# A state-space stage on one core, its hand-written order of operations sorted anew

## The chip, the cores and the metric

The kernel runs on one core of one Trainium2 chip. The metric is device time in microseconds (us), the median of the runs. Lines (L531) are those of the kernel's source. Engines: PE is TensorE (PEld its weight loads), DVE VectorE, ACT ScalarE, POOL GpSimd, SP SyncE, which here only issues DMAs.

## What is computed

A trunk of two layers on x (1 x 512 x 1024, float32): one state-space layer with a GLU and an MLP with squared ReLU, then shared keys, values and forget gates, one attention layer, a second MLP and a final norm. Only the first part matters here:

```python
def s5_mixer(u, log_dt, a_re, a_im, b_re, b_im, c_re, c_im, d_skip, w_glu):
    ...
    lam = lax.complex(a_re.astype(f32), a_im.astype(f32))
    dt = jnp.exp(log_dt.astype(f32))[:, None]
    lam_bar = jnp.exp(lam * dt)
    b = lax.complex(b_re.astype(f32), b_im.astype(f32))
    b_bar = ((lam_bar - 1.0) / lam)[..., None] * b
    bu = jnp.einsum('blgc,gpc->blgp', uf.astype(jnp.complex64), b_bar)
    a_elems = jnp.broadcast_to(lam_bar, bu.shape)
    _, states = lax.associative_scan(_ssm_binop, (a_elems, bu), axis=1)
    c = lax.complex(c_re.astype(f32), c_im.astype(f32))
    y = jnp.real(jnp.einsum('blgp,gcp->blgc', states, c))
    y = y + d_skip.astype(f32).reshape(N_GROUPS, SSM_GROUP) * uf
    z = jax.nn.gelu(y.reshape(bsz, length, D_MODEL)).astype(u.dtype)
    zw = z @ w_glu
    val, gate = zw[..., :D_MODEL], zw[..., D_MODEL:]
    return val * jax.nn.sigmoid(gate)
```

There are 64 groups of 16 channels with 64 complex states each.

## The kernel before

The sequence is cut into 64 chunks of T = 8 tokens, the 64 groups into 8 blocks of 8 groups. For each block b the kernel makes two weight matrices, runs the scan over the chunks, and adds a Toeplitz product for what happens inside a chunk. The operations have short names, and a string, ORDER (L37), lists them as name_block; a loop at L745 to 748 calls them in that order. The whole stage lies in a manual schedule over all five engines (L174), so each engine, SP and POOL with their DMA queues too, takes its own instructions exactly in the order of the string. An engine whose next instruction waits stands still, and so does all that is queued behind it.

The operations of a block, with the engine that runs each:

- win1, win2 (DVE, L531 and L536): two multiplies of 128 x 1024. wina (POOL, L345): an accumulating DMA of 512 KB adds the second onto the first (tile Win). wo1, wo2, woa: the same for the output weights (tile TW). win2 and wo2 need XY with its halves swapped, which sw does (SP, two DMAs, L341 and L342). gR and a gain on POOL (L460) scale XY first.
- pw (PE, L580): Win transposed; wt (ACT, L353): copied out of PSUM as WinT.
- u (PE, L564): the scaled input transposed; us (ACT, L353): copied to Uall. xs (ACT, L552) scales the input, after rxv (DVE) has made the norm's factor.
- pt (PE, L591): the taps, Win times Wout; ks (ACT): copied; kd (DVE, L603): the skip weight added; kw (SP, L607): written to DRAM; tr (SP, L613): read back, 512 KB, as a Toeplitz matrix, into the second half of TW.
- tab0 (DVE, L362), tab3 (ACT, L368 to L373, six instructions): tables of cosine and sine.
- pd (PE, L627): input to the states; ds, cos (DVE, L637 and L633): rotation; da (POOL): two accumulating DMAs of 128 KB onto cc; scan (DVE, L647; its factors from dec, ACT and POOL); P1, P2 (DVE, L655 and L652): rotation back; padd (POOL): two accumulating DMAs of 128 KB.
- py1 (PE, L663): Toeplitz part, needs tr; py2 (PE, L663): state part, needs padd and Wout. gelu (ACT, L678), zt (PE, L684), zh (ACT), lo (DVE, L697): activation, transpose, and a split into a high and a low part for the GLU.
- gl (SP, L113), gs (ACT, L124), gv (DVE, L128): load and split of a piece of w_glu; gp (PE, L731): six matmuls of the GLU. The rest of the GLU (L810) comes behind the stage.
- Once each: kz, dl, gnl (SP: zeros, and gains; gnl loads the four norm gains that gn transposes on PE), tk, ta, dg (DVE).

Buffers tie the blocks together. TW lives in slots of a pool with two tags, A and B, of two buffers each; the string WQ says which tag each new TW, and then gs_2 and gs_1, takes. A slot is free again only when py2 of the block that had it is done, so the wo1 of a later block waits for the py2 of an earlier one. Win has three buffers, tB two for each kind, PSUM eight of one bank (pool ps), used by pw (2), pt (2), pd, py, zt, u and each started GLU chunk (2).

```python
            for o in ORDER.split():
                f, *args = o.split("_")
                e = {"V": {"e": V}, "G": {"e": G}, "S": {"e": S}}.get(f[-1], {}) if f not in OPS else {}
                OPS[f[:-1] if e else f](*map(int, args), **e)
```

The old order works on the blocks as 0, 1, 2 and 4, 3, 5, 7, 6; block 6 is the last whose tables (tab3_6) and reload (tr_6) are made. At the start it does sw, the multiplies of blocks 0 to 2 and two loads of w_glu ahead of gnl, and the first wina is behind woa_1 on POOL.

Of the kernel before, what the change touches and what calls it, by code (L numbers as in the profile page):

```python
# [32 lines left out]
MAGIC = 12582912.0  # L33
TWO_PI = 2.0 * math.pi
CFG = dict(seq=['sfoqlantpx', 'soflntapxq'], pat=[2, 1, 1, 1, 1, 1, 1, 1, 1, 1, 1, 1, 1, 1, 1, 1, 1, 1, 1, 1, 1, 1, 1, 1, 1, 1, 1, 1, 1, 1, 1, 1, 1, 1, 0, 2, 1, 1, 1, 1, 1, 1, 1, 1, 1, 1, 1, 1, 1, 1, 1, 1, 1, 1, 1, 1, 1, 1, 1, 1, 1, 1, 2, 1, 1, 1], nl=4, nt=1, u0=66, ns=[], wk=4, st=['f u02 u03 u10 u11 u12 s u13 c0 c1', 't t u02 f t u03 u10 u11 t u12 u13 s c0 c1'], x='GGGGGGGGGGVbb', m0=3)
WQ = "AABBBABABA"
ORDER = """  # L37
LR mR dl_0 kz gR dl_1 rxv decS_0 sw_2_0 sw_2_1 win1V_2 xsS_0_1 gl_1 win1V_0 gl_2 xsS_1_0 sw_0_1 wo2V_0 gnl
wo2V_1 xsS_1_1 win2V_1 gl_0 xsS_0_0 tk u_3 u_6 u_2 taV gn usS_6 u_0 tab0V_0 usS_3 u_1 tab0V_2 usS_0 u_4
tab0V_1 u_5 tab3_2 u_7 wo1V_1 win2V_0 woa_1 wo1V_4 wina_0 usS_5 win1V_1 usS_4 tab3_0 wo1V_2 wina_1 wo1V_0  # L40
wo2V_3 woa_0 pw_0 win2V_4 usS_7 usS_1 dg wtS_0 pt_1 win2V_2 tab3_1 tab0V_3 wina_2 pw_1 tab0V_4 wo2V_2 pt_0
win1V_5 woa_2 wtS_1 pd_0 win1V_4 ksS_0 tab0V_5 wina_4 pd_1 ksS_1 ds_0 cos_0 tab3_3 kd_0 da_0 pw_2 cos_1 kw_0
wo2V_4 pt_2 kd_1 woa_4 win2V_3 kw_1 tr_0 pw_4 wtS_2 win1V_3 scan_0 wina_3 wtS_4 tr_1 P1V_0 decS_1 pd_4 ds_1
ksS_2 P2V_0 da_1 py1_0 tab3_4 wo2V_7 padd_0 kd_2 pt_4 win2V_5 kw_2 win2V_7 wina_5 py1_1 ksS_4 ds_4 tr_2 pw_3
cos_4 usS_2 kd_4 da_4 scan_1 gs_0 pd_2 tab3_5 P1V_1 P2V_1 py2_0 cos_2 padd_1 gv_0 kw_4 py1_2 wo1V_3 gelu_0
pw_5 ds_2 woa_3 tr_4 win2V_6 decS_2 da_2 zt_0 py2_1 zhS_0 win1V_7 wtS_5 lo_0 wina_7 gelu_1 pd_5 wo1V_5 wtS_3
scan_2 zt_1 py1_4 zhS_1 P2V_2 P1V_2 decS_4 pd_3 lo_1 padd_2 scan_4 pw_7 decS_3 P1V_4 pt_3 P2V_4 wtS_7 ds_3
padd_4 cos_3 gp_0_0 ksS_3 cos_5 da_3 kd_3 gp_0_1 wo2V_5 kw_3 win1V_6 py2_2 woa_5 tab0V_7 wina_6 tr_3 pd_7
gelu_2 wo1V_6 tab3_7 ds_5 zt_2 py2_4 scan_3 da_5 P1V_3 pt_5 P2V_3 wo1V_7 padd_3 py1_3 ksS_5 ds_7 woa_7 zhS_2
kd_5 pw_6 cos_7 kw_5 decS_5 da_7 lo_2 wtS_6 py2_3 scan_5 tr_5 gelu_4 pd_6 P2V_5 P1V_5 gelu_3 wo2V_6 padd_5  # L50
zt_4 gs_2 zt_3 tab0V_6 pt_7 zhS_3 woa_6 gv_2 zhS_4 py1_5 lo_3 ksS_7 lo_4 gp_0_2 tab3_6 kd_7 kw_7 gp_0_3 py2_5
tr_7 pt_6 gelu_5 ds_6 gp_2_0 cos_6 da_6 gp_2_1 gs_1 ksS_6 gv_1 zt_5 gp_2_3 zhS_5 kd_6 kw_6 gp_1_0 decS_6 lo_5
scan_6 gp_1_2 tr_6 P2V_6 decS_7 gp_1_1 P1V_6 gp_2_2 padd_6 scan_7 py1_7 P2V_7 P1V_7 py1_6 padd_7 gp_1_3 py2_6
py2_7 gelu_6 zt_6 gelu_7 zhS_6 zt_7 lo_6 zhS_7 lo_7
"""


def body(tc, x, mix_norm, mlp_norm, mlp_w1, mlp_w2, log_dt, a_re, a_im, b_re, b_im,
# [4 lines left out]
    with ExitStack() as ctx:  # L63
# [74 lines left out]
        with ExitStack() as s5c:  # L138
# [374 lines left out]
            W, glu = {}, {}  # L513
            wqk = iter(WQ)

# [1053 lines left out]
```

## Time and profile before

| | |
|---|---|
| median of 3 runs | 1218.62 us (1217.38 to 1219.13) |
| profiled execution | 1225.04 us, span of the core's instructions 1223.3 us |
| PE busy | 1123.5 us (92%), PEld 1000.2 us (82%) |
| DVE busy | 913.9 us (75%) |
| ACT busy | 610.2 us (50%) |
| POOL busy | 295.5 us (24%) |
| granted TensorE clock, mean | 0.968 |
| DMA queues, share of 16 engines | SP's 32.5%, POOL's 6.1% |

Busy shares are means over the whole span; the stage that the change touches is the first seventh of it. The profiled execution is 1.7 us longer than its span. Times in the rows are us from the span's start.

### The profile page before, as it was taken

What the parts mean: (1) busy time and instruction counts of PE and PEld (TensorE: products, weight loads), DVE (VectorE), ACT (ScalarE), POOL (GpSimd) and SP (SyncE); (2) the same over time, 40 slices, a digit from 0 to 9 for tenths busy, and PEclk for the clock granted to TensorE, in tenths of its full rate; (3) what the DMA queues carried; (4) which work ended last, traced back from release to release, by engine and by line L of the source; (5) the groups of instructions that cost most, each with busy time, mean ns of one, the idle gap of its engine ahead of it and who ended that gap; (6) DMA issues with size and microseconds to landing.
All of it is one profiled execution on the core that took longest, in us unless ns stands there. A gap on an engine that the chain in (4) does not pass through costs nothing.

```text
span 1223.3 us, 19032 instructions
## 1 busy us (share of the span) xinstructions
PE 1123.5 (92%) x7189; PEld 1000.2 (82%) x7189; DVE 913.9 (75%) x1639; ACT 610.2 (50%) x1108; POOL 295.5 (24%) x298
## 2 busy tenths in 40 slices
PE   1467789999999999999999999888899999999997
PEld 1456678899898999988888999867799999898986
DVE  8766546879977787777755788884999877778754
ACT  5673736545444344434544666553664434344433
POOL 5133313422212212110302222222422121212101
PEclk9977889999999999999999999898899999999999
DMA  6887864314323232334235433421133323323222
GB/s 136 182 172 130 157 148 130 102 53 138 121 87 121 87 120 88 103 105 123 70 103 139 105 104 104 121 70 35 52 111 114 120 87 108 100 90 113 82 97 69
DMA packets 109388, 131.37 MB, mean 107 GB/s; under 512 B 9360, under 2 KB 87984, under 8 KB 109296
## 3 DMA queue, kind: packets, MB, share of 16 engines
q1 hardware_dynamic: 104432, 117.57, 32.5%
q0 software_dynamic: 4864, 12.59, 6.1%
q8 instruction: 57, 0.93, 0.3%
q14 instruction: 35, 0.29, 0.1%
HBM read 103.21 MB, written 2.74 MB: 87 GB/s over the span
## 4 chain that ended last, share of the span: by engine, by line
PE 79%; DMA 7%; DVE 6%; ACT 4%; issue 2%; SPq 2%; POOL 1%; DVEq 0%; ACTq 0%; POOLq 0%
PE pu L919 26%; PE po L810 15%; PE pvs L1484 14%; PE pk L810 6%; PE pv L810 5%; DMA TW<-kd 3%; PE pvs L1130 2%; PE po L1268 2%; DMA kd<-ks 1%; PE pt L591 1%; PE pf L1118 1%; PE ptp L1234 1%; DMA bc<-in_ssm_b_im_dram 1%; DVE prob L1229 1%; PE pd L627 1%
## 5 line engine op out<-in xcount | busy, mean ns | idle before, releaser
L919 PE MATMUL pu<-hm,ar 128*128 128x256 f32 x1536 | 229.8, 285 | 3.2 <-ACT hm L863 2.2
L919 PEld LDWEIGHTS pu<-hm,ar 128*128 128x128 f32 x1536 | 205.3, 194 | 4.5 <-ACT hm L863 2.6
L124 ACT ACTIVATE wt<-st 128x1024 fp32r<-128x1024 f32 x110 | 116.3, 1057 | 129.3 <-PE po L810 30.5
L810 PE MATMUL po<-at,wt 128*128 128x512 f32 x768 | 176.9, 389 | 0.0
L898 POOL TENSOR_TENSOR ar<-ar,st 128x256 f32<-128x256 f32 x62 | 72.6, 1173 | 429.7 <-DVE ar L894 400.5
L1484 PE MATMUL pvs<-wt,at 128*128 128x512 f32 (+1 forms) x768 | 175.5, 388 | 0.0
L810 PEld LDWEIGHTS po<-at,wt 128*128 128x128 f32 x768 | 143.2, 188 | 29.1
L1484 PEld LDWEIGHTS pvs<-wt,at 128*128 128x128 f32 x768 | 142.6, 188 | 28.8
L128 DVE TENSOR_TENSOR wt<-st,wt 128x1024 fp32r<-128x1024 f32 x90 | 117.2, 1303 | 35.4 <-ACT wt L124 35.4
L919 PE MATMUL pu<-hd,x 128*128 128x256 f32 x768 | 137.0, 286 | 0.0
L887 ACT ACTIVATE ar<-ar 128x512 fp32r<-128x512 f32 x128 | 77.0, 627 | 92.2 <-PE pu L919 84.7
L919 PEld LDWEIGHTS pu<-hd,x 128*128 128x128 f32 x768 | 114.2, 194 | 2.7 <-issue 0.5
L888 DVE TENSOR_TENSOR ar<-ar 128x512 fp32r<-128x512 f32 x128 | 87.9, 692 | 31.4 <-ACT ar L887 31.4
L887 ACT ACTIVATE x<-st 128x512 fp32r<-128x512 f32 x62 | 36.2, 624 | 98.3 <-PE pvs L1484 49.7
L128 POOL TENSOR_TENSOR wt<-st,wt 128x1024 fp32r<-128x1024 f32 x20 | 48.1, 2407 | 145.3 <-ACT wt L124 127.2
L894 DVE TENSOR_TENSOR ar<-st 128x512 f32<-128x512 f32 x62 | 52.0, 841 | 32.8 <-DMA st<-in_mlp_w_dram 32.1
L810 PE MATMUL pv<-zt,wt 128*128 128x512 f32 x312 | 72.9, 392 | 0.3 <-ACT hT L992 0.3
L810 PEld LDWEIGHTS pv<-zt,wt 128*128 128x128 f32 x312 | 58.0, 188 | 12.4 <-ACT hT L992 0.6
L1220 ACT ACTIVATE prob<-psx,mx 128x128 f32<-128x128 f32 (+1 forms) x64 | 33.8, 528 | 60.9 <-DVE mx L1218 60.9
L899 POOL TENSOR_TENSOR ar<-ar,st 128x256 f32<-128x256 f32 x62 | 60.3, 975 | 4.2
L1039 ACT ACTIVATE at<-c 128x512 fp32r<-128x512 f32 x64 | 39.7, 630 | 40.4 <-DVE c L1037 40.4
L1025 DVE TENSOR_TENSOR hT<-hT,po 128x512 f32<-128x512 f32 x64 | 43.4, 679 | 14.8 <-PE po L810 14.8
(333 smaller groups left out, 2057.0 us busy)
## 6 DMA issues: line engine op xcount, KB each, us to landing
st<-in_mlp_w_dram SPq DMA_DIRECT2D x126, 512.0 KB, 3.5
st<-in_ssm_w_glu_dram SPq DMA_DIRECT2D x16, 512.0 KB, 6.7
st<-in_w_kvf_dram SPq DMA_DIRECT2D x14, 512.0 KB, 3.6
hx<-kt SPq DMA_DIRECT2D x48, 128.0 KB, 2.3
TW<-tB POOLq DMA_DIRECT2D x8, 512.0 KB, 6.4
Win<-tB POOLq DMA_DIRECT2D x8, 512.0 KB, 9.2
TW<-kd SPq DMA_DIRECT2D x8, 512.0 KB
st<-in_attn_wq_dram SPq DMA_DIRECT2D x8, 512.0 KB, 3.4
```

Of the source, the lines that this page charges most:

```text
L124: S.activation(wt[:, 0], st, AF.Copy)
L128: (G if slot[1] == "A" and CFG["x"][7 + lows[0] % 3] == "G" else V).tensor_tensor(wt[:, 1], st, wt[:, 0].bitcast(F32), op=ALU.subtract)
L810: TE.matmul(pts[m], wt[:, a, k, m * P:(m + 1) * P], acts[k0 + k][:, b], start=(first and k0 == parts[0][0] and k == 0 and n == 0), stop=(k ...
L887: S.activation(X[0], src, AF.Copy)
L888: V.tensor_tensor(X[1], src, X[0].bitcast(F32), op=ALU.subtract)
L894: V.tensor_tensor(Ta[:, :, js].rearrange("p w j n -> p j w n"), f[:, :, 1:3], f[:, :, 0:1].broadcast_to([P, 2, 2, P]), op=ALU.add)
L898: e.tensor_tensor(Tb[:, 0, js], Ta[:, 0, js], v[:, :, 1, 0], op=ALU.add)
L899: e.tensor_tensor(Tb[:, 1, js], Tb[:, 0, js], v[:, :, 1, 1], op=ALU.add)
L919: TE.matmul(self.acc[p], self.W[p][:, a, j], self.H.moving(p, j, b), start=(p == g[0] and j == 0 and n == 0), stop=(p == g[-1] and j == 3 ...
L1025: V.tensor_tensor(hT[:, m, :], hT[:, m, :], po[j], op=ALU.add)
L1039: S.activation(at_[:, 0], c, AF.Square)
L1484: TE.matmul(po[:, cols], A[k][:, b], wts[k // 2][:, a, k % 2, cols], start=start and n == 0, stop=stop and n == 3 * len(ks) - 1)
```

## The change

The string ORDER is replaced by another arrangement of the same operations, each of them once, and WQ by another row of the same ten letters. Nothing else differs. In the new order kz and gnl come first on SP, win2_0, win1_0 and wina_0 first on DVE and POOL, and the blocks go 0 to 7 in their own order (with small exchanges of neighbours, such as wt_5 ahead of wt_4). All tables are made by the time of ks_4; usS_6 and usS_7 come just ahead of tab3_5; the last block is 7 in every kind of operation. On DVE, 11 multiplies and 3 table adds come ahead of cos_0 and ds_0.

```diff
-WQ = "AABBBABABA"
+WQ = "AABBABABAB"
-LR mR dl_0 kz gR dl_1 rxv decS_0 sw_2_0 sw_2_1 win1V_2 xsS_0_1 gl_1 win1V_0 gl_2 xsS_1_0 sw_0_1 wo2V_0 gnl
-wo2V_1 xsS_1_1 win2V_1 gl_0 xsS_0_0 tk u_3 u_6 u_2 taV gn usS_6 u_0 tab0V_0 usS_3 u_1 tab0V_2 usS_0 u_4
-tab0V_1 u_5 tab3_2 u_7 wo1V_1 win2V_0 woa_1 wo1V_4 wina_0 usS_5 win1V_1 usS_4 tab3_0 wo1V_2 wina_1 wo1V_0
-wo2V_3 woa_0 pw_0 win2V_4 usS_7 usS_1 dg wtS_0 pt_1 win2V_2 tab3_1 tab0V_3 wina_2 pw_1 tab0V_4 wo2V_2 pt_0
-win1V_5 woa_2 wtS_1 pd_0 win1V_4 ksS_0 tab0V_5 wina_4 pd_1 ksS_1 ds_0 cos_0 tab3_3 kd_0 da_0 pw_2 cos_1 kw_0
-wo2V_4 pt_2 kd_1 woa_4 win2V_3 kw_1 tr_0 pw_4 wtS_2 win1V_3 scan_0 wina_3 wtS_4 tr_1 P1V_0 decS_1 pd_4 ds_1
-ksS_2 P2V_0 da_1 py1_0 tab3_4 wo2V_7 padd_0 kd_2 pt_4 win2V_5 kw_2 win2V_7 wina_5 py1_1 ksS_4 ds_4 tr_2 pw_3
-cos_4 usS_2 kd_4 da_4 scan_1 gs_0 pd_2 tab3_5 P1V_1 P2V_1 py2_0 cos_2 padd_1 gv_0 kw_4 py1_2 wo1V_3 gelu_0
-pw_5 ds_2 woa_3 tr_4 win2V_6 decS_2 da_2 zt_0 py2_1 zhS_0 win1V_7 wtS_5 lo_0 wina_7 gelu_1 pd_5 wo1V_5 wtS_3
-scan_2 zt_1 py1_4 zhS_1 P2V_2 P1V_2 decS_4 pd_3 lo_1 padd_2 scan_4 pw_7 decS_3 P1V_4 pt_3 P2V_4 wtS_7 ds_3
-padd_4 cos_3 gp_0_0 ksS_3 cos_5 da_3 kd_3 gp_0_1 wo2V_5 kw_3 win1V_6 py2_2 woa_5 tab0V_7 wina_6 tr_3 pd_7
-gelu_2 wo1V_6 tab3_7 ds_5 zt_2 py2_4 scan_3 da_5 P1V_3 pt_5 P2V_3 wo1V_7 padd_3 py1_3 ksS_5 ds_7 woa_7 zhS_2
-kd_5 pw_6 cos_7 kw_5 decS_5 da_7 lo_2 wtS_6 py2_3 scan_5 tr_5 gelu_4 pd_6 P2V_5 P1V_5 gelu_3 wo2V_6 padd_5
-zt_4 gs_2 zt_3 tab0V_6 pt_7 zhS_3 woa_6 gv_2 zhS_4 py1_5 lo_3 ksS_7 lo_4 gp_0_2 tab3_6 kd_7 kw_7 gp_0_3 py2_5
-tr_7 pt_6 gelu_5 ds_6 gp_2_0 cos_6 da_6 gp_2_1 gs_1 ksS_6 gv_1 zt_5 gp_2_3 zhS_5 kd_6 kw_6 gp_1_0 decS_6 lo_5
-scan_6 gp_1_2 tr_6 P2V_6 decS_7 gp_1_1 P1V_6 gp_2_2 padd_6 scan_7 py1_7 P2V_7 P1V_7 py1_6 padd_7 gp_1_3 py2_6
-py2_7 gelu_6 zt_6 gelu_7 zhS_6 zt_7 lo_6 zhS_7 lo_7
+LR mR kz gnl win2V_0 win1V_0 decS_0 dl_1 rxv wina_0 gl_1 sw_2_0 gn win2V_1 xsS_1_1 dl_0 gR sw_2_1 xsS_0_1 tk
+sw_0_1 wo2V_0 gl_2 xsS_1_0 gl_0 pw_0 wo2V_1 wo1V_0 u_3 wtS_0 u_6 dg u_2 xsS_0_0 woa_0 u_7 wo1V_2 wo1V_1 usS_2
+u_5 u_0 usS_5 taV woa_1 u_1 usS_0 u_4 tab0V_2 usS_1 pd_0 tab0V_0 usS_4 gs_0 tab0V_1 win1V_1 tab3_0 pt_0 wo2V_2
+wina_1 gv_0 woa_2 win2V_3 ksS_0 cos_0 tab3_2 ds_0 kd_0 da_0 wo2V_4 kw_0 win1V_3 pw_1 win1V_2 wina_3 tab3_1
+pt_1 win2V_2 wo2V_3 wina_2 tab0V_3 scan_0 wtS_1 tr_0 pd_1 P1V_0 decS_1 P2V_0 ksS_1 wo1V_3 padd_0 pw_3 tab3_3
+ds_1 cos_1 woa_3 kd_1 win1V_5 kw_1 pw_2 da_1 win2V_4 usS_3 wtS_2 pt_2 win2V_5 wtS_3 tab0V_7 wina_5 py1_0
+win1V_4 ksS_2 tab0V_5 wina_4 py2_0 tab3_7 kd_2 tab0V_4 kw_2 wo2V_5 pd_2 tr_1 wo1V_4 pd_3 ds_2 woa_4 gelu_0
+scan_1 pt_3 cos_2 decS_2 cos_3 da_2 tab3_4 zt_0 P2V_1 pw_5 win1V_6 win2V_6 tr_2 P1V_1 wina_6 tab0V_6 padd_1
+win2V_7 zhS_0 ksS_3 lo_0 wtS_5 py1_1 kd_3 kw_3 wo2V_6 tab3_6 pw_4 ds_3 pd_5 scan_2 da_3 P1V_2 wtS_4 py1_2
+P2V_2 decS_3 padd_2 pd_4 usS_6 usS_7 tab3_5 pt_4 cos_4 tr_3 py2_1 win1V_7 wina_7 pw_6 ds_4 ksS_4 wo1V_5 da_4
+py2_2 wtS_6 kd_4 scan_3 kw_4 gelu_1 woa_5 pd_6 P1V_3 P2V_3 gelu_2 zt_1 cos_5 padd_3 py1_3 zhS_1 wo1V_6 decS_4
+lo_1 pw_7 woa_6 gp_0_0 wtS_7 ds_5 tr_4 scan_4 da_5 pd_7 P1V_4 decS_5 gp_0_1 P2V_4 cos_6 padd_4 pt_5 wo2V_7
+zt_2 ksS_5 py2_3 zhS_2 kd_5 kw_5 pt_6 wo1V_7 gelu_3 lo_2 woa_7 zt_3 ksS_6 py1_4 zhS_3 kd_6 kw_6 ds_6 lo_3 da_6
+py2_4 scan_5 tr_5 gp_0_3 gelu_4 P2V_5 gs_2 P1V_5 pt_7 cos_7 padd_5 decS_6 gv_2 tr_6 zt_4 ksS_7 gp_2_0 zhS_4
+kd_7 ds_7 gp_2_1 da_7 lo_4 gp_2_3 kw_7 scan_6 py1_5 P1V_6 decS_7 P2V_6 py2_5 padd_6 py1_6 gelu_5 gs_1 scan_7
+zt_5 tr_7 gp_2_2 zhS_5 gv_1 gp_0_2 P2V_7 P1V_7 gp_1_0 lo_5 padd_7 py2_6 gp_1_2 gelu_6 zt_6 py1_7 zhS_6 lo_6
+gp_1_1 py2_7 gp_1_3 gelu_7 zt_7 zhS_7 lo_7
```

## Rows read from the trace of the kernel before

**Rows 1.** Busy time of each engine by stretch: busy (x), granted clock, DMA share, GB/s.

```profile
core 0: us, PE busy (x) PEld busy (x) DVE busy (x) ACT busy (x) POOL busy (x), PEclk, DMA share, GB/s
32.00:175.00 143.00, 98.36 (x995) 83.87 (x996) 87.34 (x111) 81.06 (x127) 41.32 (x55) 0.86 0.79 155
64.00:90.00 26.00, 15.76 (x154) 13.91 (x154) 15.59 (x22) 19.11 (x30) 10.32 (x14) 0.74 0.92 175
175.00:252.00 77.00, 76.74 (x364) 63.90 (x363) 52.35 (x61) 41.86 (x69) 25.14 (x23) 1.00 0.39 124
252.00:1223.00 971.00, 943.40 (x5796) 848.08 (x5794) 748.38 (x1366) 469.95 (x878) 213.04 (x177) 0.98 0.32 98
```

**Rows 2.** Chain of waits, end of the stage: start, us, what.

```profile
153.79 5.42 DMA kd<-ks
...
159.27 7.87 DMA TW<-kd
...
167.28 1.97 PE py L663 x32
...
174.72 2.27 PE pv L810 x9
...
196.04 50.16 PE pv L810 x220
```

**Rows 3.** Groups of instructions, 0 to 180 us: busy us, mean ns, idle before.

```profile
L591 PE MATMUL pt<-TW,Win 128*16 128x128 f32 x128 | 19.7, 321 | 2.3 <-DMA TW<-tB 1.7 <-ACT cs L372 0.5
L731 PE MATMUL pv<-zt,wt 128*128 128x512 f32 x72 | 19.2, 420 | 0.0
L627 PE MATMUL pd<-Uall,WinT 128*128 128x64 f32 x128 | 18.9, 312 | 2.0 <-ACT WinT L353 2.0
L663 PE MATMUL py<-TW,Uall 128*64 128x64 f32 x256 | 12.5, 270 | 24.3 <-DMA TW<-kd 24.3
L580 PE MATMUL pw<-ident,Win 128*128 128x128 f32 x64 | 10.8, 325 | 4.0 <-ACT cs L368 3.0 <-DMA Win<-tB 1.0
L531 DVE TENSOR_TENSOR TW<-LL,XY 128x1024 f32<-128x1024 f32 x8 | 9.8, 1221 | 1.8 <-PE pu L564 1.6 <-PE py L663 0.2
L353 ACT ACTIVATE ks<-pt 16x512 f32<-16x512 f32 x16 | 9.0, 582 | 8.3 <-PE pt L591 8.2
L678 ACT ACT_TABLE_LOAD x3 | 3.8, 1283 | 0.1
L372 ACT ACT_TABLE_LOAD x2 | 2.6, 1283 | 0.0
```

**Rows 4.** Timeline of SP: start us, us, engine and line, what.

```profile
26.15 0.52 SPq L341 DMA_DIRECT2D XY<-XY  x1
...
30.95 0.53 SPq L341 DMA_DIRECT2D XY<-XY  x1
```

**Rows 5.** Timeline of the other engines up to 84 us, same columns, idle before.

```profile
34.27 2.36 DVE L536 TENSOR_TENSOR tB<-LL,XY 128x1024 f32<-128x1024 f32 x2 [3.77 <-DMA XY<-XY]
44.28 0.86 POOL L345 DMA_DIRECT2D Win<-tB  x1
62.65 0.69 DVE L637 SCALAR_TENSOR_TENSOR dt<-pd,cs 128x512 f32<-128x512 f32 x1 [0.17 <-PE pd L627]
72.88 0.63 ACT L368 ACTIVATE cs<-cs 128x512 f32<-128x512 f32 x1
...
76.01 0.80 ACT L373 ACTIVATE cs<-cs,sg 128x512 f32<-128x512 f32 x1
83.08 0.57 ACT L353 ACTIVATE Uall<-pu 128x512 f32<-128x512 f32 x1
```

**Rows 6.** Timeline of DVE and PE, 119 to 163 us.

```profile
120.14 1.23 DVE L531 TENSOR_TENSOR TW<-LL,XY 128x1024 f32<-128x1024 f32 x1 [0.20 <-PE py L663]
...
124.36 1.22 DVE L531 TENSOR_TENSOR TW<-LL,XY 128x1024 f32<-128x1024 f32 x1
161.71 1.15 PE L663 MATMUL py<-TW,Uall 128*64 128x64 f32 x32
```

**Rows 7.** DMA issues of the page: KB each, median us from issue to landing.

```profile
TW<-tB POOLq DMA_DIRECT2D x8, 512.0 KB, 6.4
```

## The prediction, made before the changed kernel ran

> **What bounds the kernel now.** I read first how busy each engine is, stretch by stretch, then the chain of waits, then the timeline of the first 175 us, which is all that the change touches. From 175 us to 252 us PE is busy 76.74 of 77 us (the GLU's matmuls), and from there to the end 943 of 971 us [rows 1]. So the second part is PE's own length, and what the state-space stage gains or loses reaches the end one for one. In the stage itself nothing is full: from 32 to 175 us PE is busy 98 of 143 us, DVE 87, ACT 81, POOL 41, and the DMA engines 0.79, with 0.92 in the best stretch [rows 1]. A stage in which every resource has room is bound by waits, and the order decides the waits. The chain shows the last of them: kd at 153.79 takes 5.42 us to DRAM, the Toeplitz reload 7.87 us, py1_6 starts at 167.28, and the GLU's own matmuls begin at 174.72 [rows 2]. This was block 6, whose tables, kernel taps and reload the old order does last of all, after block 7's.
>
> **What the change does.** It adds and drops no operation: 12 GLU pieces, 16 accumulating DMAs of 512 KB, 8 reloads on both sides. The letters of WQ follow the new order of the Wout tiles: nothing by themselves. Two ACT table loads may go: ACT now switches between Sin and Gelu five times [rows 3], in the new order three times (gelu_0, back for tab3_4, gelu_1), 2 x 1.28 us. They are inside the sum of ACT below.
>
> **Start.** SP must first wait for POOL's gain; it issues the first swap at 26.15, and a swap was waited for 3.3 us after its issue (30.95 to 34.27) [rows 4, 5]. win2V_0, now at the head of DVE, so starts at 29.5 (bounds: a landing of 2 to 6 us, 28 to 32). Two multiplies later (1.22 us each [rows 3]) POOL issues wina_0, at 31.9 instead of 44.28 [rows 5]: the first transfer of the blocks starts 12 us earlier. What that costs: rxv, and with it the 16 xs copies on ACT, wait behind these multiplies. That is covered, because before the Uall copies had to wait on gn anyway, whose loads SP issued after the swaps and two w_glu loads; now gnl is ahead of all but kz. Without that cover it costs the 6 us or so by which rxv moves.
>
> **First scan input.** Before, ds_0 starts at 62.65 [rows 5]. The new DVE queue has 6 multiplies fewer ahead of it (7.3 us), 3 table adds of half that size fewer (1.8 us), and gv_0 more (1.2 us): 54.8 with the old waits, 51 without any. I take 53.5, with ACT's tab3_0 just done.
>
> **Middle.** From there ACT holds the pace. Until wtS_4 its queue has 6 tab3 at 3.9 us (72.88 to 76.81 [rows 5]), 23.4; four ks and five wt at 1.2 (two copies each, like those of ks [rows 3]), 10.8; dec_1, dec_2, us_3, gelu_0 and zh_0 at about 0.7, 3.6; two table loads, 2.6. Sum 40.4, done at 93.9. PE then does pd_4, pt_4 and py2_1: 2.4, 2.5 and 1.6 (busy time of each group divided by 8 blocks [rows 3]), 6.5: 100.4. That frees a slot for wo1V_5. From py2_1 to py2_3 PE's queue holds two pw (1.4 each), two pd (4.7), one pt (2.5), two gp (3.2), three py (4.7) and two zt (0.7 each, half a pw): 19.3. At 119.7 py2_3 frees the slot for wo1V_7, which ran at 124.36 before [rows 6].
>
> **Last block.** From wo1V_7 the chain is woa_7, pt_7, ks_7, kd_7, kw_7, tr_7, py1_7: 37.35 us before (124.36 to 161.71 [rows 6]). The parts alone are woa at 6.4 [rows 7], pt 2.5, ks 1.2, kw 5.42 and the reload 7.87 [rows 2]: 23.4 us. The old lap also held woa_7 in POOL's queue behind other transfers and kw_7 behind ACT's tab3_6 path; in the new order all tables are done by then. I take 33, nearer the measured lap than the bare parts. After it come py1_7, one gp and py2_7, 4.8 us (block 6 no longer stands between). End of the stage: 119.7 + 33 + 4.8 = 157.5 instead of 174.72, **17 us less**. With 23.4 it is 27 us, with 37.35 it is 13.
>
> **The DMA queue as a check.** From 32 to 175 us the DMA engines worked 0.79 x 143 = 113 us [rows 1]. The new order starts at about 32 too: at 0.92 it cannot end before 155, at 0.90 it ends at 157.5, at 0.79 at 175. So 17 us need the best stretch's density all along; this caps the gain at 20 us or so, and is where it can be lost.
>
> POOL's 512 KB took 6.4 us in the median from issue to landing [rows 7]. The Trainium skill (DMA: Bandwidth & Descriptors, Anatomy of one DMA) gives such a DMA about 2 us plus its bytes over 436 GB/s; an estimate from that page is 3.2 us for woa and for the reload and 2.2 for kw. By it the bare parts would be 12 us, the end at 137 and the gain 38 us. The row decides against it.
>
> **Waits that are new.** On POOL, da_2 stands behind the memset of dec_2, which on ACT stands behind gelu_0, which needs py2_0; wina_6, padd_1 and da_3 queue behind it. py2_0 follows padd_0 and tr_0; with ds_0 at 53.5 and kd_0 just after it, kw_0 and tr_0 (5.42 and 7.87) end near 68 and py2_0 near 72, while ACT comes to gelu_0 near 75: 3 us of cover, and beyond it ACT and POOL lose one for one. On SP, tr_1 stands behind kw_2, and tr_5 behind kw_6. tr_1 then goes out near 73 and lands near 81; py1_1 comes after pw_5 on PE, about 79, so 2 us may be lost there, which the wait for wtS_4 hides.
>
> **Behind the stage.** SP, POOL and the GLU's weight loads keep their work; DMA share there is 0.39 [rows 1], so the weights come in time for a GLU that starts earlier, and PE has no room there to lose the gain. The profiled execution took 1225.04 us, 6.4 above the median of the runs; I take the 17 us off the median, 1218.62: **1201 us**.
>
> **Rivals.**
> 1. The DMA engines are the bound. For it: the share of 0.92 at 64 to 90 us [rows 1], where DVE and PE had room. Moving wina_0 forward puts it beside the w_glu loads, and woa, wina, da and padd share POOL's one queue. (The Trainium skill, the same page, Issuing engines are not separate DMA queues: transfers that SP and POOL issue run on the same 16 engines and interleave. The trace agrees as far as 0.92 goes.) At a share of 0.83 the stage ends at 32 + 113 / 0.83 = 168: 7 us less, 1212.
> 2. It changes nothing that can be measured: 0.79 is what these transfers reach with such latencies, and the end stays at 175. A measurement of this kernel tells about 0.2% (2.4 us) from no change. 1218.6.
> 3. It is slower: PSUM. The pool has 8 buffers. The new order transposes u_6 and u_7 early on PE and copies them (usS_6, usS_7) only behind tab3_6, wtS_4 and decS_3, past 90 us by the ACT sum; before, one such buffer stayed that long (copied at 83.08 [rows 5]). Six buffers then serve pw (2), pt (2), pd, py and zt, and gp_0, which holds two, comes 13 us earlier. If PE stands still for a buffer that ACT frees only behind a wait for PE, each lap of a slot grows. The old order's longest, wo1V_6 at 120.14 to 174.72, is 54.6 us [rows 2, 6]; with the early lead eaten (wo1V_7 at 124.4) the stage ends at 179 and the kernel at 1223. It decides once py1_1 starts later than about 100 us.
> 4. More than I think: the lap near its bare 23.4 us, 1191.
>
> **Chances.** My forecast (1192 to 1208) 0.57; rival 1 (1208 to 1216) 0.19; rival 2 0.07; rival 3 0.13; rival 4 (under 1192) 0.04. Faster by over 0.2%: 0.80; within: 0.07; slower: 0.13. The range runs from just above the short lap, 1192, through rival 1 and a little into no change, 1217; it leaves out rivals 3 and 4 and about half of rival 2.
>
> **What would show it.** Right: wina_0 issued near 32, the first dt near 53 to 55, ACT's last tab3 before 100, wo1V_7 (the last TW multiply) between 113 and 122, py1_7 the last reload's reader, and PE's first GLU matmul outside the stage (line 810) near 157. Two ACT table loads fewer. From there to the end the same length as before. Wrong: a first dt after 60; idle time of PE in front of pw, pt or py put down to an ACT copy (rival 3); or scans idle behind the cc transfers with a DMA share over 0.9 and an end past 165 (rival 1).

## The result, and the profile after

The changed kernel took 1204.69 us in the median of 10 runs (1199.35 to 1211.47), the kernel before 1219.66 in 10 runs beside them (1213.08 to 1228.59): ratio 0.9869, 95% interval 0.9837 to 0.9901. A second measurement, beside other runs of before, gave 0.9876 (0.983 to 0.9922). Forecast were 17 us less; by these ratios it was 15 to 16. The medians differ by 15.0 and 14.7 us.

The profiled execution of the changed kernel took 1199.35 us (span 1197.6), the shortest of its ten runs, while that of before, 1225.04, lies near the top of what that kernel's ten runs span. The two traces therefore differ by more than the medians, and I keep to what they show about places. Busy time by stretch, in the columns of [rows 1]:

```profile
core 0: us, PE busy (x) PEld busy (x) DVE busy (x) ACT busy (x) POOL busy (x), PEclk, DMA share, GB/s
32.00:158.00 126.00, 102.06 (x1024) 87.83 (x1025) 88.58 (x113) 83.55 (x132) 40.42 (x54) 0.85 0.84 173
64.00:90.00 26.00, 20.57 (x243) 18.53 (x242) 19.47 (x26) 23.91 (x38) 8.71 (x12) 0.83 0.96 183
158.00:235.00 77.00, 75.85 (x380) 63.96 (x378) 54.49 (x64) 42.57 (x73) 30.49 (x28) 1.00 0.36 113
235.00:1197.00 962.00, 935.79 (x5751) 840.41 (x5749) 741.30 (x1360) 465.73 (x869) 207.68 (x172) 0.99 0.33 99
```

The stage holds the same work in less time: PE is busy 102 of 126 us, where it was 98 of 143. Behind it hardly anything has changed. From the start of the long run of 220 GLU matmuls to the end of the span it is 1025.2 us here and 1027.3 before [rows 2]; in all 14 profiles of this study it lies between 1022.8 and 1027.7. The start of that run is therefore my measure of the stage: 172.43 instead of 196.04.

What PE waited for from 30 to 155 us (in all, how often, the longest):

```profile
engine line waited for: us in total, times, longest us
PE pw L580 <- DMA Win<-tB: 11.3, 2, 8.2
PE py L663 <- ACT ks L353: 5.4, 1, 5.4
PE py L663 <- DMA P<-P: 5.2, 2, 3.2
PE pw L580 <- ACT Uall L353: 2.2, 1, 2.2
PE pd L627 <- ACT WinT L353: 2.1, 1, 2.1
PE pt L591 <- DMA TW<-tB: 2.1, 2, 1.2
PE py L663 <- DMA TW<-kd: 1.5, 1, 1.5
```

The last line is the one to see. Before, PE stood 24.3 us in front of py1 because the Toeplitz reload TW<-kd had not landed [rows 3]; now 1.5. The reload of block 6 is no faster (10.52 us below, 7.87 before [rows 2]). What changed is the distance: from a block's kd to its py1 it is 14.5 to 24.1 us now and was 10.9 to 19.7, longer for every block, and the string puts 92 operations of PE between pt and py1, summed over the blocks, where it put 70. Block 0 is the exception: it has six on both sides. Its wait of 6.36 us for the reload is gone too, but PE now waits 3.06, 2.13 and 2.20 us in front of pw_1, pd_1 and pw_2, which stand between its pt and its py1.

The reloads are not the whole difference. All of PE's waits from 30 to 182 us add up to 51.4 us before and 30.0 now, 21.4 less. Two more waits of the kernel before, both at the start, are gone (its profile, same window):

```profile
PE pg L705 <- DMA gl<-in_mlp_norm_dram: 9.3, 1, 9.3
PE pu L564 <- ACT xs L552: 8.0, 1, 8.0
```

In their place PE waits 8.2 us for the Win of block 0 (pw_0), and the waits for ACT's ks and for P are new or longer.

The timeline of the places that the forecast named (wina_0, ds_0, the end of tab3_6 and wt_4, py2_1, wo1_7, py1_7):

```profile
27.84 1.06 POOL L345 DMA_DIRECT2D Win<-tB  x1 [1.57 <-DVE rxa L486]
...
47.54 0.68 DVE L637 SCALAR_TENSOR_TENSOR dt<-pd,cs 128x512 f32<-128x512 f32 x1
...
86.06 0.80 ACT L373 ACTIVATE cs<-cs,sg 128x512 f32<-128x512 f32 x1
86.76 1.05 ACT L353 ACTIVATE WinT<-pw 128x512 f32<-128x512 f32 x2
...
92.40 1.15 PE L663 MATMUL py<-TW,P 128*64 128x64 f32 x32
...
115.64 1.23 DVE L531 TENSOR_TENSOR TW<-LL,XY 128x1024 f32<-128x1024 f32 x1 [0.78 <-PE py L663]
...
149.21 1.15 PE L663 MATMUL py<-TW,Uall 128*64 128x64 f32 x32
```

And the end of the chain of waits (start, us, what):

```profile
117.16 5.24 DMA TW<-tB
...
124.14 10.52 DMA TW<-kd
...
134.79 1.98 PE py L663 x32
...
146.12 2.72 PE pv L810 x12
...
149.28 1.08 PE py L663 x32
...
154.61 3.63 PE pv L810 x16
...
172.43 50.16 PE pv L810 x220
```

woa_7 lands, the reload of block 6 follows, and py1_6 at 134.79 is PE's last wait of the stage. From there PE works without a gap; py1_7 at 149.21 waits for its place in the queue and not for its reload, which went out at 136.0. Twelve matmuls of the rest of the GLU (L810) already run at 146.12, ahead of py1_7; in the old order none runs inside the stage. The steady GLU matmuls begin at 154.61 instead of 174.72 [rows 2], with those twelve done.

### The profile page after: what moved, and what is told of

The parts are those of the page before. It is cut to its first block, busy times and chain, and to the rows that moved or that the text cites. A ratio compares the mean times of both kernels' runs of the same rounds, so it can differ in the third digit from the quotient of the medians.

```text
span 1197.6 us, 19030 instructions
## 1 busy us (share of the span) xinstructions
PE 1119.2 (93%) x7189; PEld 996.8 (83%) x7189; DVE 912.1 (76%) x1639; ACT 607.8 (51%) x1106; POOL 291.2 (24%) x298
## 4 chain that ended last, share of the span: by engine, by line
PE 79%; DVE 8%; DMA 5%; ACT 3%; issue 3%; SPq 0%; POOL 0%; DVEq 0%; ACTq 0%; POOLq 0%
PE pu L919 25%; PE po L810 16%; PE pvs L1484 14%; PE pk L810 6%; PE pv L810 6%; PE pvs L1130 2%; PE po L1268 2%; DMA cc<-dt 1%; PE ptp L1234 1%; PE pf L1118 1%; DMA TW<-tB 1%; DVE prob L1229 1%; DMA bc<-in_ssm_b_im_dram 1%; DMA TW<-kd 1%; PE pv L731 1%
## 5 line engine op out<-in xcount | busy, mean ns | idle before, releaser
L810 PE MATMUL po<-at,wt 128*128 128x512 f32 x768 | 176.9, 389 | 0.0
L810 PEld LDWEIGHTS po<-at,wt 128*128 128x128 f32 x768 | 143.2, 188 | 29.1
L128 DVE TENSOR_TENSOR wt<-st,wt 128x1024 fp32r<-128x1024 f32 x90 | 117.1, 1302 | 27.9 <-ACT wt L124 27.7
L128 POOL TENSOR_TENSOR wt<-st,wt 128x1024 fp32r<-128x1024 f32 x20 | 48.2, 2408 | 143.6 <-ACT wt L124 125.5
L810 PE MATMUL pv<-zt,wt 128*128 128x512 f32 x312 | 72.4, 391 | 0.2 <-ACT hT L992 0.2
L810 PEld LDWEIGHTS pv<-zt,wt 128*128 128x128 f32 x312 | 58.2, 188 | 12.3 <-ACT hT L992 0.4
```

The source lines that it names most:

```text
L128: (G if slot[1] == "A" and CFG["x"][7 + lows[0] % 3] == "G" else V).tensor_tensor(wt[:, 1], st, wt[:, 0].bitcast(F32), op=ALU.subtract)
L810: TE.matmul(pts[m], wt[:, a, k, m * P:(m + 1) * P], acts[k0 + k][:, b], start=(first and k0 == parts[0][0] and k == 0 and n == 0), stop=(k ...
```

## The experiments

All are edits of ORDER unless said otherwise. "Long run" is the start of the 220 matmuls in the one profile of each kernel, the ratio is to the kernel before, beside it on the same chip. The medians of before in the three later sets were 1222.93, 1219.96 and 1221.79 us, so compare ratios, not medians, across sets. The same kernel (changed, and again) gave long runs of 172.43 and 184.03 in its two profiles; a difference of that size between two rows says nothing by itself.

| kernel | median us | ratio, 95% interval | long run |
|---|---|---|---|
| before | 1219.66 | 1 | 196.04 |
| changed | 1204.69 | 0.9869 (0.9837 to 0.9901) | 172.43 |
| changed, again | 1205.28 | 0.9876 (0.983 to 0.9922) | 184.03 |
| old order, new head | 1221.15 | 0.9986 (0.9958 to 1.0014) | 198.30 |
| new order, late head | 1212.19 | 0.9918 (0.9886 to 0.9951) | 186.57 |
| woa_6, woa_7 on DVE | 1201.66 | 0.9833 (0.9793 to 0.9873) | 174.68 |
| middle additions on DVE | 1205.87 | 0.9873 (0.9827 to 0.9919) | 176.29 |
| scaling of XY on DVE | 1199.87 | 0.9835 (0.9805 to 0.9865) | 172.62 |
| us_6, us_7 early | 1204.24 | 0.986 (0.9817 to 0.9902) | 181.23 |
| table of block 7 late | 1204.05 | 0.9862 (0.9826 to 0.9897) | 176.32 |
| old order, taps of 6 early | 1223.73 | 1.0023 (1.0 to 1.0046) | 197.07 |
| old order, scaling on DVE | 1220.09 | 0.9994 (0.9965 to 1.0023) | 192.53 |
| scaling and woa_6, woa_7 on DVE | 1202.62 | 0.9839 (0.9806 to 0.9873) | 173.63 |
| the same, table of 7 late | 1200.90 | 0.983 (0.9797 to 0.9864) | 177.01 |

**1. The new head in the old order.**

```diff
-LR mR dl_0 kz gR dl_1 rxv decS_0 sw_2_0 sw_2_1 win1V_2 xsS_0_1 gl_1 win1V_0 gl_2
+LR mR kz gnl win2V_0 win1V_0 dl_0 gR dl_1 rxv wina_0 decS_0 sw_2_0 sw_2_1 gn win1V_2 xsS_0_1 gl_1 gl_2
...
```

Further down, pw_0 stands ahead of u_3 and wtS_0 ahead of usS_6, and the old places of what moved are empty.

> The old order with only the head of the new one: zeros and gain loads first on SP, win2_0, win1_0 and wina_0 first, gn, pw_0 and wt_0 early. The rest, block 6 last and its tables last, is the old order. Read by the start of the long run of 220 GLU matmuls (196.04 before, 172.43 in the changed kernel). Theory A, the early start is carried to the end: first dt at about 53 and the long run at 184 to 188, 8 to 12 us less. Theory B, as the prediction's sum has it, the last block's lap and the place of block 6 make most of the gain: the first dt is early but the wait moves to the old tail, long run at 191 to 196, 0 to 5 us less. Theory C, the DMA engines are the bound: the same bytes start up to 12 us earlier and end 5 to 10 us earlier.

Nothing was gained (0.9986), though wina_0 went out at 30.52 and not at 44.28 [rows 5]. First row of PE's waits, then the timeline:

```profile
PE py L663 <- DMA TW<-kd: 26.3, 6, 8.4
PE pt L591 <- DMA Win<-tB: 8.9, 1, 8.9
```

```profile
30.52 1.06 POOL L345 DMA_DIRECT2D Win<-tB  x1 [5.36 <-DVE Win L531]
...
53.73 1.65 PE L591 MATMUL pt<-TW,Win 128*16 128x128 f32 x7 [8.93 <-DMA Win<-tB]
...
62.93 0.69 DVE L637 SCALAR_TENSOR_TENSOR dt<-pd,cs 128x512 f32<-128x512 f32 x1 [0.17 <-PE pd L627]
...
109.37 1.98 PE L663 MATMUL py<-TW,Uall 128*64 128x64 f32 x32 [6.99 <-DMA TW<-kd]
```

The old order puts pt_1 ahead of pt_0 and pd_0 on PE. pt_1 now waits 8.93 us for block 1's Win, and ds_0 runs at 62.93, where it always did (62.65 [rows 5]). Theories A and C fall for the old order, and B with them in part: not even the first dt came early. The last line is py1_4, which waits 6.99 us for its reload.

**2. The late head in the new order.**

```diff
-LR mR kz gnl win2V_0 win1V_0 decS_0 dl_1 rxv wina_0 gl_1 sw_2_0 gn ...
+LR mR decS_0 dl_1 rxv gl_1 sw_2_0 ...
...
```

Further down, kz and gnl stand behind gl_2, gn behind u_2, win2V_0 and win1V_0 behind wo1V_1, wina_0 behind woa_1, pw_0 behind u_4 and wtS_0 behind usS_1.

> The changed kernel with a late head: zeros and gain loads behind the last w_glu load but one on SP, gn behind u_2, win2_0 and win1_0 behind wo1_1, wina_0 behind woa_1, pw_0 and wt_0 behind the u and us of blocks 0 to 4. All else is the new order. Theory A (the start is carried to the end): wina_0 8 to 12 us later and the long run 8 to 12 us later than in the changed kernel, 181 to 185. Theory B (order of the later blocks and the last lap): 172 to 177, at most 5 us of the 23 lost. Theory C (DMA engines the bound): 176 to 182, since woa_1 and others fill the time in which wina_0 waits.

Ratio 0.9918: the order behind the head alone is worth about 10 us against before, and the head about 6 us more on top of it (its interval just overlaps with that of the changed kernel). wo1_7 and py1_7:

```profile
129.66 1.22 DVE L531 TENSOR_TENSOR TW<-LL,XY 128x1024 f32<-128x1024 f32 x1 [0.78 <-PE py L663]
...
163.34 1.15 PE L663 MATMUL py<-TW,Uall 128*64 128x64 f32 x32
```

wo1_7 is 5 us later than in the kernel before (124.36 [rows 6]), yet the long run starts 9.5 us earlier. From wo1_7 to the long run it is 56.9 us here, 56.8 in the changed kernel and 71.7 before [rows 2, 6]; over all profiles, 54 to 62 in the ten of the new order and 69 to 73 in the four of the old. So in the new order the head moves wo1_7, and the order of the later blocks shortens what follows. The long run, 186.57, lies just beyond the 181 to 185 of theory A, but the changed kernel's own second profile has 184.03; by the ratios the head is worth less than A had it.

This run and the one before it complete a square. PE's waits from 30 to 182 us:

| head, order behind it | on reloads, us | all, us | median, us |
|---|---|---|---|
| old, old (before) | 24.3 | 51.4 | 1219.66 |
| new, old (1) | 26.3 | 50.8 | 1221.15 |
| old, new (2) | 1.9 | 40.7 | 1212.19 |
| new, new (changed) | 1.5 | 30.0 | 1204.69 |

The waits on reloads go with the order behind the head, whatever the head. The new head takes another 11 us of waits away, and only in the new order. These are single profiles (the changed kernel's second has 0 and 35.1 us), so the pattern counts and not the tenths.

**3. Two late additions on DVE.**

```diff
-woa_6 ... woa_7
+woaV_6 ... woaV_7
```

> The changed kernel with the two Wout additions of blocks 6 and 7 done by DVE in place of POOL's accumulating DMAs: 1 MB less through the DMA engines, two DVE operations of 1.2 us more, in the last third of the stage. If the last lap is on the path (the prediction's sum: woa_7, 6.4 us of latency, is part of it): pt_7 starts up to 4 us earlier and the stage ends 2 to 4 us earlier. If PE's queue alone is the bound there (PE has no gap from 134.79 on): 0 to 1 us. If DVE is: up to 2 us later.

Ratio 0.9833. pt_7 did not start earlier (125.5 against 122.54 in the changed kernel's first profile; its second has 135.7), and the long run, 174.68, is no better than in that first profile. Its six times stay close (1199.50 to 1203.31), but the interval overlaps with that of the changed kernel: inconclusive, at best 4 us.

**4. Three additions of the middle on DVE.**

```diff
-wina_4 ... wina_5 ... woa_4
+winaV_4 ... winaV_5 ... woaV_4
```

> The changed kernel with three additions of the middle (wina_4, wina_5, woa_4) done by DVE in place of accumulating DMAs: 1.5 MB less in the stretch 64 to 90 us, where the DMA engines showed a share of 0.96, and 3.6 us more of DVE there. By the engines' time per byte over the stage a 512 KB transfer is about 2.7 us of all 16 engines, so 8 us of DMA time go. Theory C (the DMA engines bound this stretch): da_2 lands 4 to 8 us earlier (86.66 in the changed kernel) and the stage ends 3 to 8 us earlier. Theory B (ACT and PE pace the middle): share falls to 0.75 to 0.85 in 64 to 90 and the end moves by less than 2 us either way.

```profile
64.00:90.00 26.00, 16.89 (x182) 14.32 (x183) 22.87 (x28) 19.25 (x30) 5.23 (x8) 0.76 0.59 119
```

The DMA share of this stretch fell from 0.96 to 0.59, and da_2 took 5.3 us from its issue to its landing where it took 11.5. The time did not move (0.9873). The engine that took the work, DVE, is busy 22.87 of 26 us there, and da_2 was issued 6 us later, so it landed where it had landed before, at 86.67. The DMA engines are nearly full in this stretch, but freeing them at DVE's cost buys nothing. What it would be worth without that cost, this edit does not show.

**5. The changed kernel again, and the first scaling of XY on DVE.** The second is one argument, ahead of the stage's list:

```diff
-            gain(GA)
+            gain(GA, V)
             sw(0, 0)
```

> The changed kernel once more, beside the next three. In the profiles so far POOL's scaling of XY (line 460) took 0.73 to 0.82 us where it began before 20.5 us, and 4.1 to 5.2 us where it began after 20.9, with DVE's run of multiplies beside it. If that is a matter of when the input's last load lands and not of the order, this profile may show either form; where it shows the long one the first swap goes out near 25 and the long run of 220 GLU matmuls begins 2 to 6 us later than 172.43.

> The changed kernel with the first scaling of XY (line 460, 128 x 256) done by DVE in place of POOL. If POOL's long form (4 to 5 us against 0.7) comes from DVE's multiplies beside it, and if the lead of the head is carried to the end: the first swap goes out by about 21.5 in every run, the highest times of the changed kernel (up to 1211) go, and the median falls by 2 to 4 us against the changed kernel beside it. If the head is not on the path, no difference.

Timeline of the scaling (L460), of some of DVE's operations beside it and of the first swap, first in the changed kernel's first profile, then in its second, then with the scaling on DVE:

```profile
20.23 0.73 POOL L460 TENSOR_TENSOR XY<-XY,gbc 128x256 f32<-128x256 f32 x1 [1.68 <-ACT XY L333]
20.27 0.83 DVE L476 TENSOR_TENSOR tmp<-LL,cr 128x128 f32<-128x128 f32 x1
20.98 0.52 SPq L341 DMA_DIRECT2D XY<-XY  x1
21.02 0.28 DVE L478 TENSOR_TENSOR ML<-ML,tmp 128x128 f32<-128x128 f32 x1
```

```profile
20.38 1.02 DVE L467 TENSOR_TENSOR LL<-tmp 128x384 f32<-128x384 f32 x2
...
20.77 4.03 POOL L460 TENSOR_TENSOR XY<-XY,gbc 128x256 f32<-128x256 f32 x1 [2.72 <-ACT XY L333]
...
23.66 0.55 DVE L480 TENSOR_TENSOR ML<-ML,tmp 128x384 f32<-128x384 f32 x1
...
24.83 0.52 SPq L341 DMA_DIRECT2D XY<-XY  x1
```

```profile
21.09 0.42 DVE L460 TENSOR_TENSOR XY<-XY,gbc 128x256 f32<-128x256 f32 x1 [0.36 <-ACT XY L333]
21.55 0.52 SPq L341 DMA_DIRECT2D XY<-XY  x1
```

The same kernel shows both forms, so the short one is not the order's doing: it is the run's. POOL starts when ACT's copy of XY is done. Whether that falls ahead of the beginning of DVE's run of 128 x 384 multiplies or behind it is a matter of some tenths of a microsecond, and then the first swap goes out at 21 or at 25. In the second profile wina_0 is 2.3 us later, ds_0 4 us and the long run 11.6 us, where 2 to 6 were expected; what makes 11.6 of 4 was not followed up. With the scaling on DVE the six times lie between 1199.21 and 1203.08, where the changed kernel beside it spread from 1199.35 to 1215.30: the long times are gone, as expected. The median is 5.4 us lower, more than the 2 to 4 expected, but the two intervals overlap.

**6. us_6 and us_7 early (PSUM).**

```diff
-... ksS_0 cos_0 ... decS_3 padd_2 pd_4 usS_6 usS_7 tab3_5 ...
+... ksS_0 usS_6 usS_7 cos_0 ... decS_3 padd_2 pd_4 tab3_5 ...
```

> The changed kernel with usS_6 and usS_7 behind ks_0 in place of behind decS_3: two PSUM buffers come free 35 us earlier. If PSUM holds PE back (rival 3 of the prediction; in the changed kernel py1_1 waited 5.43 us for ACT's copy ks_3): that wait goes, py2_1 ends 2 to 5 us earlier and the stage 2 to 4 us. If ACT paces the middle, the wait moves behind wt_5 and wt_4 and the end stays within 1 us. The copies cost ACT 1.2 us ahead of tab3_2 and give them back later.

Ratio 0.986, no difference. py1_1 no longer waits for ks_3's copy, so those 5.4 us were a wait for a PSUM buffer. In its place it waits 3.59 us for its reload; the wait has in part changed its name.

**7. The table of block 7 late.**

```diff
-... py2_0 tab3_7 kd_2 ... gelu_4 P2V_5 gs_2 P1V_5 ...
+... py2_0 kd_2 ... gelu_4 P2V_5 gs_2 tab3_7 P1V_5 ...
```

> The changed kernel with the table of block 7 (tab3_7, 3.9 us on ACT) behind gs_2 in place of behind ks_2: as in the old order, the last block's table comes at the end, with two more ACT table loads (2 x 1.28 us). If ACT paces the middle: py2_1 ends 3 to 4 us earlier. If the old order's end was long because its last table came late: ks_7, kd_7 and kw_7 go back by 4 to 6 us and the stage ends 2 to 5 us later. If PE's own queue is the bound at the end, the two cancel: within 2 us.

Ratio 0.9862, no difference. The waits of ACT from 46 to 100 us say why:

```profile
ACT dec L353 <- DVE tz L647: 4.9, 2, 4.1
ACT WinT L353 <- PE pw L580: 3.8, 2, 3.6
```

With 3.9 us taken from ACT's queue, gelu_0 ran at 76.9 and not at 80.7 (second profile of the changed kernel, which has the same long scaling). Then dec_2 waited 4.1 us for scan_1, because dec has one buffer, and wt_4 ended at 95.4 against 95.6. Up to wt_4, ACT and the path of the scans are equally long there. Behind wt_4 this profile is ahead all the same: py2_1 came at 99.17 against 105.47, more than the 3 to 4 us expected, and the long run 7.7 us earlier. But the four times (1202.60 to 1204.11) are no better than the changed kernel's, whose own two profiles differ by more than that, so only the part up to wt_4 is read here.

**8. The taps of block 6 early in the old order.**

```diff
-... wo1V_7 padd_3 ... woa_7 ... wo2V_6 ... pt_7 zhS_3 woa_6 ... ksS_7 ... kd_7 kw_7 ... tr_7 pt_6 ... ksS_6 ... kd_6 kw_6 ... tr_6
+... wo1V_7 wo2V_6 padd_3 ... woa_7 woa_6 ... pt_7 pt_6 ... ksS_7 ksS_6 ... kd_7 kd_6 kw_7 kw_6 ... tr_7 tr_6
```

> The old order with the taps of block 6 (wo2_6, woa_6, pt_6, ks_6, kd_6, kw_6, tr_6) each put right behind those of block 7, its table left where it was. If, as the prediction's sum has it, block 6 standing behind block 7 costs the end of the old order about 8 us: tr_6 goes out some 5 us behind tr_7 instead of 10 us, the long run of GLU matmuls begins 4 to 9 us before 196, and the time falls by 4 to 9 us. If the table of block 6 is the binding part, the scan of block 6 (ds_6 at 149) keeps the end: 0 to 3 us. If the end is set by PE's own work, nothing.

Ratio 1.0023: nothing gained, perhaps 3 us lost. tr_6 went out at 149.0 instead of 159.27 [rows 2] and py1_6 ran 3 us earlier. The end of the chain of waits:

```profile
149.47 10.88 DMA cc<-dt
...
160.47 1.24 DVE tz L647
...
163.07 1.23 DVE tz L647
...
166.66 6.13 DMA P<-P
...
172.93 1.97 PE py L663 x32
```

A second chain, from the late table of block 6 over ds_6 (which waited 5.1 us for it, at 147.37), da_6, the scans and padd_7, ends where the reload's ended. It also became longer: da_6 goes out at 149.0 beside tr_7 (148.3) and tr_6 (149.0) and lands 11.4 us later; before it was 7.1 us.

**9. The scaling on DVE in the old order.** The edit of 5 on the kernel before.

> The old order with the first scaling of XY done by DVE in place of POOL. The head alone brought the old order nothing, so the first swap goes out 4 us earlier and the time stays within 2 us of the old order's. If the old order's scatter of 15 us between runs is also the long and the short form of that scaling, its times close up as those of the new order did, to within 6 us.

Ratio 0.9994. ds_0 ran 4.3 us earlier, at 58.36. PE's waits and the timeline at py1_4:

```profile
PE py L663 <- DMA TW<-kd: 28.0, 7, 8.1
```

```profile
105.16 1.98 PE L663 MATMUL py<-TW,Uall 128*64 128x64 f32 x32 [7.97 <-DMA TW<-kd]
```

py1_4 ran at 105.70 before with 6.14 us of waiting; the lead of 4.3 us has shrunk to 0.5 there, and the waits on reloads grew by 3.7 us (24.3 [rows 3]). The old order's own times still spread over 9 us (1214.99 to 1223.84), so most of its scatter is not this scaling.

**10. The edits that seemed to help, together.** The scaling and woa_6, woa_7 on DVE; then the late table besides (the diffs of 5, 3 and 7).

> The changed kernel with both edits that helped: the first scaling of XY on DVE and the additions woa_6 and woa_7 on DVE. If they act at different places (start, last lap) they add: 1197 to 1199, against 1199.87 with the scaling alone and 1201.66 with the additions alone. If the additions only helped where the start was late: 1200, no better than the scaling alone.

> The kernel with the scaling of XY and woa_6 and woa_7 on DVE, and the table of block 7 behind gs_2 besides. If ACT paces the middle also with the early start: py2_1 3 to 4 us earlier than without it and, if the last lap has room for the late table, an end 1 to 3 us earlier. If the last lap has none, 0 to 3 us later.

0.9839 and 0.983: no better than the scaling alone (0.9835) as far as the intervals tell. They do not add. In the last one dec_2 waits for scan_1 again, 4.3 us.

## Why the prediction was right, point by point

**Total and sign.** 17 us forecast, 15 to 16 measured. The terms were less exact than the sum, and that the sum fits so well is in part luck: the start came earlier than forecast, the middle ran longer than forecast, the wait that shrank most was no term at all, and the forecast end of the stage, 157.5, lies between the 154.61 and 166.21 at which the steady GLU matmuls begin in the two profiles of the changed kernel. The direction and the two places of the gain, the head and the part behind wo1_7, were right.

**What bounds the stage.** "Waits, and the order decides" holds as far as 4, 6 and 7 go: each took work or a wait from one resource, and none gained time by it. But I read the chain of waits only at its end and missed its largest repeated term, the 24.3 us of PE in front of py1, though it stands in [rows 3]. In all four profiles of the old order PE waits 23.8 to 28.0 us on reloads, in all ten of the new order 0 to 3.6. That the old order swallows a lead in these waits is what 9 shows at py1_4. That they go with the order behind the head is what 1 and 2 show; that they are what its 10 us are made of is read from the traces and not shown by an edit, for whether the gain comes back if py1 alone is moved back in the old order was not tried.

**Start.** The step that failed in size: win2V_0 was forecast at 29.5 from the swap's issue at 26.15 and its landing. It ran at 25.2 in the first profile and at 27.5 to 27.7 in the three of the new order with the new head and the long scaling. I took POOL's 5.2 us for fixed; it has two forms (5). In the short form the swap is not even the last thing that win2V_0 needs: DVE's own run before it ends at 25.25, and win2V_0 follows it without idle time. So the short form is worth 2.3 us there and not the 4 us by which the swap goes out earlier.

**First scan input.** 53.5 forecast, 47.54 measured, 51.6 in the second profile. The multiplies were counted rightly, but started earlier.

**Middle.** The sum for ACT, 40.4 us, measured 41.7 from the end of tab3_0 (46.15) to that of wt_4 (87.81). pd_4, pt_4 and py2_1: 6.5 against 5.7. From py2_1 to py2_3: 19.3 against 22.1, of which 3.2 is a wait for padd_2. wo1_7 came at 115.64 and in the second profile at 123.98; the forecast, 119.7, lies between. That ACT alone "holds the pace" is not what 7 shows: up to wt_4 the scans' path is as long.

**Last block.** 33 us taken for the lap, 33.6 measured (36.8 in the second profile). The 4.8 us behind py1_7 left out gp_1_3, which is in the queue there too; measured were 5.4. But it is PE's queue that fills its last 14 us, not the latencies that I listed. And "block 6 no longer stands between" is not a term of its own: 8 shows that in the old order two chains, its reload and its table, ended together, so undoing one gives nothing. The whole part from wo1_7 on, forecast 12.6 us shorter, came out 14.9 shorter up to the long run and 11.4 up to the steady GLU matmuls (the twelve that ran ahead of py1_7 make 2.7 us of that difference).

**Parts as terms of a sum.** The forecast's 4.7 us ahead of wo1_7 and 12.6 behind it look like the 6 us of the head and the 10 us of the order behind it (2), but that is not the same division: with the late head wo1_7 came 5 us later than before, and what follows it made up for that and more. Nor are the two independent: the new head is worth nothing in the old order (1), and so is the faster scaling (9).

**New waits.** da_2 behind dec_2 behind gelu_0 is there: issued at 75.16, landed at 86.66. No py1 waited for tr_1 or tr_5; the one reload that PE waited for is tr_6, 1.5 us.

**Rivals.** Rival 1: the share did reach 0.96 where I expected it, but in 4 it fell to 0.59 and the time stayed; my cap of 20 us by a share of 0.92 was too low a density (the share was about 1.0 from 32 to 80 us, and 1.01 from 64 to 80 us in the kernel before). Rival 2: the 0.2% that I wanted to tell from no change was too fine; the intervals here are 0.3% either way. Rival 3: the PSUM wait exists, 5.43 us at py1_1, at 81.5 and not past 100, and costs nothing that can be measured (6).

**What was to show it.** Two ACT table loads fewer (1106 instructions of ACT against 1108), the last tab3 done at 94.04, py1_7 the last reload's reader, the same length behind the stage: right. wo1_7 within 113 to 122: right in the first profile (115.64), not in the second (123.98). wina_0 near 32 and a first dt at 53 to 55: wrong, both earlier in both profiles. PE's first matmul of line 810 near 157: it came at 146.12, ahead of py1_7, and the steady ones at 154.61.

## What to carry to other kernels

In an order that is fixed for each engine, look first for the wait that repeats on the busiest engine, here PE in front of its reloads, and ask what else it could run meanwhile. A lead at the start is worth only what the queue behind it lets through: try it alone in the old order before counting it. Where two chains end together, removing one shows nothing; the evidence is the wait that takes its place.

## What was not expected of the hardware

POOL's one multiply of 128 x 256 took 0.73 to 0.82 us in the three profiles where it began 0.09 us or more ahead of DVE's unbroken run of eight 128 x 384 multiplies and sums, and 3.84 to 5.20 us in the seven where it began from 0.03 us ahead of that run's beginning to 0.59 us behind it. In the second profile of the changed kernel the run ends at 24.21 and POOL at 24.80, 0.59 us later; in all seven POOL ends 0.58 or 0.59 us behind the last DVE instruction that it waits for (the kernel before and that of 8 have a scaling of 128 x 768 right behind the run, and there POOL waits for that too). In the short form it is DVE's operation that is stretched, in the first profile 0.83 us instead of 0.28. The Trainium skill (SBUF — State Buffer, Who interferes with whom) says that a DVE instruction with two SBUF inputs contends with a GpSimd instruction that reads SBUF, and that the order of issue decides which of two blocks. These rows agree, with one addition: POOL's wait did not end with one DVE instruction but lasted through the whole run. For this kernel it is the difference between a first swap at 21 and at 25 us, and moving that multiply to DVE (0.42 us) closed the changed kernel's times up from 16 us of spread to 4.
